# One layer of a hybrid decoder on one core: the MLP's products by one level of Strassen's scheme

## The chip, the core and the metric

The kernel runs on one core of a Trainium2 chip. The core has five engines, each with its own instruction queue, worked off in order: TensorE (PE, matrix products, results in PSUM), VectorE (DVE), ScalarE (ACT), GpSimd (POOL) and SyncE (SP), which here only issues transfers between memory and SBUF. The metric is the device time of one execution in microseconds. Before the change it is 2307.84 us (median of 3 runs, 2306.13 to 2308.58).

## The reference, cut to what matters

```
h   = layer_norm(x)                       # x: 2048 tokens x 1024
z   = h @ w_in                            # input projection, 2320 columns
mix = concat(s5(z), gla(z), rglru(z)) @ w_out
h   = layer_norm(2**0.25 * h + mix)
ff  = square(relu(h @ mlp_w1)) @ mlp_w2   # 1024 -> 4096 -> 1024
out = layer_norm(2**0.25 * h + ff)
```

All arrays are float32. The three mixers and the input projection are not touched by the change.

## The kernel before, in words

The order of every engine's work is written out by hand: the kernel builds a list of ticks (`tick`, L211), each with some matrix products of TensorE, and spreads everything else over the ticks; the emission loop (L1617) then issues it all in program order. No compiler reorders it.

A float32 product is made of three matmuls: each operand is split into a high part (a ScalarE copy to float32r) and the rest (a VectorE subtraction), and `mm3` (L219) adds high x high, high x low and low x high. One matmul has 128x128 weights and 512 moving columns. Weights come from memory in pieces, are split by `stage_weights` (L1508, ScalarE at L1526, then VectorE; instructions that an engine helper records have line 77, and those of `mm3` L221 to L223) and used at once.

After the input projection, whose ticks also hold the mixers, the 2048 tokens go in two halves of 1024 (blocks 0 and 1, then 2 and 3, of 512 tokens). For each half: the out-projection of its two blocks (`add_out_proj`, L1253, 32 ticks of 12 matmuls, banks `po`), the residual and the first LayerNorm (`ln1`, L1279), transposes of the rows through TensorE (`h1t`, L1287, `tp_h1T`), and the MLP (`add_mlp`, L1299). The MLP takes the hidden layer in blocks of 256 columns: `p1` makes 128 hidden columns for 512 tokens with 24 matmuls (banks `pz_ph`), ScalarE and VectorE apply relu and square and split the result (`hid`), and `p2` adds the block's part of the second product (banks `pf`) to the rows, which stay in SBUF as `acc`, by one VectorE addition for each bank (`add_acc`, L1338). The hidden layer never leaves SBUF. The last LayerNorm (`ln2_half`, L1408) of the first half lies in the out-projection of the second; that of the second half comes with the last two blocks of the hidden layer. In both the rows' last columns go to ScalarE and GpSimd, the others to VectorE (`NP`, `ln_apply`, L145).

All loads and stores are issued by SP in program order (`load`, L83); an issue waits until its data or its place is ready, and those behind it wait with it.

## Time and profile before

| | |
|---|---|
| median of 3 runs | 2307.84 us |
| profiled execution, span from first to last instruction | 2307.0 us |
| TensorE busy | 2204.8 us, 96%, 10688 matmuls |
| VectorE busy | 1297.4 us, 56% |
| ScalarE busy | 825.9 us, 36% |
| GpSimd busy | 312.9 us, 14% |
| mean granted clock of TensorE | 0.983 |

The profile is of one execution of its own; its span is 0.8 us under the median, and what lies around the span (start and end of the launch) is not in it. Times in a trace are microseconds from the span's start. Idle time is put down to what ended it; for an engine that is not the bottleneck it costs nothing. In a row, `x320` is a count of instructions and `out<-in` names the tiles written and read.

### The profile page before, as it was taken

The numbers are of one execution on the slowest core, as the hardware profiler recorded it, in microseconds if no ns is written. First come the engines' busy times: TensorE is split into PE (matmuls) and PEld (weight loads), VectorE is DVE, ScalarE is ACT, GpSimd is POOL, SyncE is SP. The second block draws the span as 40 slices with busy tenths as digits, with TensorE's granted clock in tenths as the row PEclk, the third lists the DMA queues.
The fourth block names the chain that finished last, engine by engine and source line by source line (L and its number), as shares of the span: only waits on it lengthen the run. The fifth ranks groups of instructions, "written<-read, shape, count | busy, mean of one in ns | idle before, by whom it ended". The sixth has DMA issues, their size and how long they took to land.

```text
span 2307.0 us, 28509 instructions
## 1 busy us (share of the span) xinstructions
PE 2204.8 (96%) x10688; PEld 1840.2 (80%) x10688; DVE 1297.4 (56%) x2210; ACT 825.9 (36%) x1629; POOL 312.9 (14%) x511
## 2 busy tenths in 40 slices
PE   6887999999999999999999999999999999999998
PEld 5776788888877778888888888877788888888886
DVE  5566865546456754445445445967544454454457
ACT  3436656667663332221221222423322212212222
POOL 5486610000002200000000000133000000000003
PEclk9998999999999999999999999999999999999999
DMA  7332354555453331111111113662311111111132
GB/s 208 102 124 77 107 178 119 129 135 135 115 169 107 99 110 55 56 41 51 55 38 55 55 37 102 197 217 69 110 55 55 44 48 55 42 51 55 39 90 105
DMA packets 245130, 212.79 MB, mean 92 GB/s; under 512 B 63856, under 2 KB 196096, under 8 KB 244992
## 3 DMA queue, kind: packets, MB, share of 16 engines
q1 hardware_dynamic: 244224, 208.87, 30.6%
q0 software_dynamic: 768, 2.11, 0.4%
q8 instruction: 84, 1.38, 0.3%
q14 instruction: 54, 0.44, 0.1%
HBM read 174.67 MB, written 36.84 MB: 92 GB/s over the span
## 4 chain that ended last, share of the span: by engine, by line
PE 75%; DVE 9%; POOL 6%; ACT 5%; DMA 2%; issue 2%; SPq 0%; POOLq 0%; DVEq 0%; ACTq 0%
PE pf L223 9%; PE pf L221 9%; PE pf L222 9%; PE pz_ph L222 9%; PE pz_ph L223 9%; PE pz_ph L221 9%; PE po L221 2%; PE po L223 2%; PE po L222 2%; POOL rs_ln L77 1%; POOL rs_in L77 1%; DVE acc L77 1%; PE pr_v L221 1%; PE pr_v L223 1%; PE pr_v L222 1%
## 5 line engine op out<-in xcount | busy, mean ns | idle before, releaser
L221 PE MATMUL pf<-w_w,hid 128*128 128x512 f32 x1024 | 401.7, 392 | 6.8 <-ACT hid L1313 6.8
L223 PE MATMUL pf<-w_w,hid 128*128 128x512 f32 x1024 | 400.8, 391 | 6.8 <-DVE hid L77 6.8
L222 PE MATMUL pf<-w_w,hid 128*128 128x512 f32 x1024 | 400.0, 391 | 1.1 <-DVE w_w L77 1.1
L221 PE MATMUL pz_ph<-act,w_w 128*128 128x512 f32 x1024 | 398.5, 389 | 0.0
L223 PE MATMUL pz_ph<-act,w_w 128*128 128x512 f32 x1024 | 398.4, 389 | 0.0
L222 PE MATMUL pz_ph<-act,w_w 128*128 128x512 f32 x1024 | 398.4, 389 | 0.0
L77 DVE TENSOR_TENSOR acc<-acc,pf 128x512 f32<-128x512 f32 x416 | 281.1, 685 | 173.7 <-PE pf L223 170.6
L1526 ACT ACTIVATE w_w<-st_w 128x512 fp32r<-128x512 f32 x320 | 191.1, 625 | 476.8 <-PE pf L223 425.9
L77 DVE TENSOR_TENSOR rl<-rl 128x512 f32<-128x512 f32 x128 | 92.7, 724 | 425.2 <-ACT hid L1313 425.0
L1312 ACT ACTIVATE rl<-pz_ph 128x512 f32<-128x512 f32 x128 | 76.4, 597 | 470.3 <-PE pz_ph L223 470.2
L77 POOL TENSOR_TENSOR rs_ln<-rs_ln,cst 128x1 f32<-128x1 f32 x32 | 35.7, 1117 | 1470.2 <-DVE rs_ln L77 1469.6
L223 PEld LDWEIGHTS pf<-w_w,hid 128*128 128x128 f32 x1024 | 193.1, 189 | 49.1 <-DVE hid L77 9.0
L221 PEld LDWEIGHTS pf<-w_w,hid 128*128 128x128 f32 x1024 | 193.3, 189 | 47.8 <-ACT hid L1313 8.1
L222 PEld LDWEIGHTS pf<-w_w,hid 128*128 128x128 f32 x1024 | 193.1, 189 | 41.3 <-DVE w_w L77 1.8
L223 PEld LDWEIGHTS pz_ph<-act,w_w 128*128 128x128 f32 x1024 | 192.2, 188 | 40.0
L221 PEld LDWEIGHTS pz_ph<-act,w_w 128*128 128x128 f32 x1024 | 192.2, 188 | 39.8
L222 PEld LDWEIGHTS pz_ph<-act,w_w 128*128 128x128 f32 x1024 | 192.2, 188 | 39.8
L77 DVE TENSOR_TENSOR w_w<-st_w,w_w 128x512 fp32r<-128x512 f32 x320 | 214.0, 698 | 11.5 <-ACT w_w L1526 10.8
L221 PE MATMUL po<-w_wo,act 128*128 128x512 f32 x256 | 104.9, 410 | 7.8 <-DVE acc L77 7.8
L223 PE MATMUL po<-w_wo,act 128*128 128x512 f32 x256 | 102.0, 398 | 0.0
L222 PE MATMUL po<-w_wo,act 128*128 128x512 f32 x256 | 101.7, 397 | 0.0
L77 DVE TENSOR_TENSOR hid<-rl,hid 128x512 fp32r<-128x512 f32 x128 | 88.5, 691 | 4.4
(358 smaller groups left out, 3442.7 us busy)
## 6 DMA issues: line engine op xcount, KB each, us to landing
st_w<-in_mlp_w_dram SPq DMA_DIRECT2D x320, 256.0 KB, 3.0
st_wo<-in_w_out_dram SPq DMA_DIRECT2D x64, 256.0 KB, 3.1
w<-s5w_d SPq DMA_DIRECT2D x16, 640.0 KB, 5.1
xr<-in_x_dram SPq DMA_DIRECT2D x16, 512.0 KB, 5.1
h_d<-xr SPq DMA_DIRECT2D x16, 512.0 KB, 4.5
mx<-mix_d SPq DMA_DIRECT2D x16, 512.0 KB, 5.4
acc<-h_d SPq DMA_DIRECT2D x16, 512.0 KB, 5.2
out_dram<-acc SPq DMA_DIRECT2D x12, 512.0 KB, 4.3
```

The costliest lines, as they stand in the source:

```text
L77: return fn(*a, **k)
L221: T.matmul(ps, lhs[0], rhs[0], start=first, stop=False)
L222: T.matmul(ps, lhs[0], rhs[1], start=False, stop=False)
L223: T.matmul(ps, lhs[1], rhs[0], start=False, stop=last)
L1312: S.activation(rl, ps, AF.Relu)
L1526: S.activation(u.tile[:, 0], st, AF.Copy)
```

## The change: what it does

Strassen's scheme (in Winograd's form) computes a product of 2x2 blocks with 7 block products in place of 8, at the price of sums of blocks before and after.

The four out-projection blocks now follow each other, then comes the whole MLP. Rows after `ln1` are stored to memory (`h1_d`). Jobs (`tjob`) load them, transpose them, form the 7 right operands of MLP 1 with ScalarE, VectorE and GpSimd, and store them (`rop_d`): 16 jobs for tokens 0 to 1023 during the out-projection, 16 more during MLP 1.

MLP 1 has 32 steps: 1024 tokens x 256 hidden columns each, 16 steps for each half of the tokens. A step has 7 products of 12 matmuls; the right operands of a half stay in SBUF (7 rings of 1 MB in memory, split once). Left operands are sums of blocks of `mlp_w1`, made by GpSimd and then split. Two or three products are added in one bank after the other, with copies (ScalarE) of the bank in between; relu and square give four blocks of the hidden layer, from which GpSimd makes sums, and 7 operands go to memory (`hid_d`).

MLP 2 has 64 parts: 8 chunks of 512 hidden rows, and in each 8 parts of 256 tokens. A part has 7 products of 6 matmuls. Its left operands are loaded from `hid_d` and split, its right ones are sums of blocks of `mlp_w2`, made and split once in a chunk. Results are added to the rows of all tokens, which lie in SBUF (`acc`, 8 tiles of 256 tokens): four additions by VectorE from PSUM, three by GpSimd from ScalarE's copies. The last LayerNorm of a tile follows its last chunk.

`V`, `G`, `S`, `T` are VectorE, GpSimd, ScalarE, TensorE; `task(n, ...)` puts work behind product n of `run`, and `evac` handles the product before.

```diff
+    o0 = len(plan)
+    hooks["op", 0] = o0
+    for b in range(4):
+        add_out_proj(b)
+    def h1_ready(b, t):
+        if t % 2:
+            z["h1", b // 2, 2 * (b % 2) + t // 2] = True
+    for t in range(4):
+        for b, n in ((1, o0 - 2), (2, o0 + 17), (3, o0 + 33)):
+            hook(n + 2 * t, mix_load, b, 2 * t)
+            hook(n + 2 + 2 * t, mix_split, b, 2 * t)
+        for b in range(4):
+            hook(o0 + 16 * b + 2 + t, acc_load, b, t)
+        for b in range(3):
+            n = o0 + 16 * b + 16 + 2 * t
+            hook_two(n, ln1, b, t, NP[4 + b % 2])
+            hook(n + 3, h1_ready, b, t)
+    hook(o0 + 1, set_gb, "gb1", ln1_g[0], ln1_b[0], "ln1")
...
-                z["accp"] = open_pool("accp", bufs=8)
+                z["accp"] = open_pool("accp", bufs=6)
                 z["gbp"] = open_pool("gbp")
-            if n == hooks["mlp", 0]:
+                z["tjp"] = open_pool("tjp")
...
+        gens = [ln1(3, t, NP[5]) for t in range(4)]
+        for g in gens:
+            next(g)
+        for g in gens:
+            for _ in g:
+                pass
+            for e in late:
+                e()
+            late.clear()
+        drain("tj0")
+        for nm in ("tjp", "gbp", "accp", "psp", "smallp", "wst", "rowp", "wp", "actp", "const"):
+            close_pool(nm)
...
+        ORDER = ("p1", "p2", "p7", "p6", "p3", "p4", "p5")
+        INDEX = {"p1": 0, "p2": 1, "p7": 2, "p6": 3, "p4": 4, "p5": 5, "p3": 6}
...
+        def split(dst_hi, dst_lo, src):
+            S.activation(dst_hi, src, COPY)
+            V.tensor_tensor(dst_lo, src, f(dst_hi), op=ALU.subtract)
...
+            def products(g, p):
+                nonlocal last
+                i = INDEX[p]
+                if p == "p1":
+                    g.bank["a"] = ps2.tile([P, BLK], F32, tag="a", name=f"pa_{g.nm}", bufs=3)
+                elif p == "p2":
+                    g.bank["b"] = ps2.tile([P, BLK], F32, tag="b", name=f"pb_{g.nm}", bufs=2)
+                elif p == "p7":
+                    g.bank["c"] = ps2.tile([P, BLK], F32, tag="c", name=f"pc_{g.nm}", bufs=2)
+                ps = g.bank["b" if p == "p2" else "c" if p in ("p7", "p4") else "a"]
+                terms = g.terms(i)
+                for k, (lhs, rhs) in enumerate(terms):
+                    mm3(ps, lhs, rhs, k == 0 and p in ("p1", "p2", "p7"), k == len(terms) - 1,
+                        p not in ("p1", "p2", "p7"))
+            def evac():
+                nonlocal last
+                if last is not None:
+                    last[0].evac(last[1])
+                last = None
+            for g in groups:
+                for p in ORDER:
+                    for e in tasks.pop((n, "before"), ()):
+                        e()
+                    who = prev if p == "p3" else g
+                    if who is not None:
+                        products(who, p)
+                    evac()
+                    if who is not None:
+                        last = who, p
+                    for e in tasks.pop(n, ()):
+                        e()
+                    n += 1
+                prev = g
+            evac()
+            products(prev, "p3")
+            prev.evac("p3")
...
+        def ring_load(sb, i):
+            rt = rings[sb][i] = ringp.tile([P, 2, 4, BLK], F32R, tag=f"ring{i}", name=f"ring_{sb}_{i}")
+            load(f(rt[:, 1]), rop_d[sb, i].rearrange("k p c -> p k c"))
+        def ring_split(sb, i, hf):
+            rt = rings[sb][i]
+            ks = slice(2 * hf, 2 * hf + 2)
+            split(rt[:, 0, ks], rt[:, 1, ks], f(rt[:, 1, ks]))
...
+            def load(self):
+                self.raw = raw_tile([P, KD, 2, P], f"w1_{self.nm}")
+                load(self.raw, w1_v[:, :, 256 * self.c:256 * self.c + 256].rearrange("p k (i c) -> p k i c", i=2))
...
+            def sum(self, which):
+                a = self.a
+                if which == 1:
+                    a["s1"] = sump.tile([P, 4, P], F32, tag="s1", name=f"s1_{self.nm}")
+                    G.tensor_tensor(a["s1"], a["21"], a["22"], op=ALU.add)
...
+            def keep(self, i, nm):
+                store(hid_d[self.sb, self.c, i], self.out[nm])
+            def copy(self, nm, ps):
+                self.out[nm] = t = cpp.tile([P, BLK], F32, tag=nm if nm == "p1" else "pu", name=f"{nm}_{self.nm}",
+                                            bufs=1 if nm == "p1" else 2)
+                S.activation(t, ps, COPY)
+            def add(self, i, nm, ps, other):
+                t = self.tile(nm)
+                V.tensor_tensor(t, ps, self.out[other], op=ALU.add)
+                V.scalar_tensor_tensor(t, t, 0.0, t, op0=ALU.max, op1=ALU.mult)
+                self.keep(i, nm)
+            def evac(self, p):
+                bank = self.bank
+                if p == "p1":
+                    self.copy("p1", bank["a"])
+                elif p == "p2":
+                    self.add(0, "c11", bank["b"], "p1")
+                elif p == "p7":
+                    self.copy("p7", bank["c"])
+                elif p == "p6":
+                    self.copy("u2", bank["a"])
+                elif p == "p4":
+                    self.add(1, "c21", bank["c"], "u2")
+                elif p == "p5":
+                    self.add(4, "c22", bank["a"], "p7")
+                else:
+                    t = self.tile("c12")
+                    S.activation(t, bank["a"], AF.Relu)
+                    S.activation(t, t, AF.Square)
+            def hsum(self, which):
+                o = self.out
+                if which == 1:
+                    G.tensor_tensor(self.tile("s1"), o["c12"], o["c22"], op=ALU.add)
+                    self.keep(5, "s1")
...
+        steps = [Step(n) for n in range(32)]
+        steps[0].load()
+        steps[1].load()
+        for i in range(7):
+            ring_load(0, i)
+        for w in (1, 3, 2):
+            steps[0].sum(w)
+        def first(i):
+            steps[0].split(i)
+            if i == 1:
+                steps[0].sum(4)
+            for hf in range(2):
+                ring_split(0, i, hf)
+        first(0)
...
+        for i, n in ((2, 0), (3, 1), (4, 2), (5, 3), (6, 5)):
+            task(n, first, i)
+        for n in range(31):
+            m = steps[n + 1]
+            b = 7 * n
+            if n:
+                task(b - 7, m.load)
+            o = 4 if n == 0 else 0
+            for w, k in ((1, 0), (3, 0), (2, 1)):
+                task(b + max(k, o), m.sum, w)
+            for i, k in ((0, 0), (1, 1)):
+                task(b + max(k, o), m.split, i)
+            task(b + max(2, o), m.sum, 4)
+            for i, k in ((2, 2), (3, 3), (4, 4), (5, 6), (6, 6)):
+                task(b + max(k, o), m.split, i)
+        for n in range(32):
+            for w, k in ((1, 5), (3, 6), (2, 6), (4, 7)):
+                task(7 * n + 7 + k, steps[n].hsum, w)
+        for i, k in enumerate((0, 1, 2, 3, 5, 6, 11)):
+            task(7 * 15 + k, ring_load, 1, i)
+            for hf in range(2):
+                task(7 * 15 + k + 5, ring_split, 1, i, hf)
...
+            def split(self, i):
+                nm = ("11", "21", "t3", "t2", "t4", "t1", "22")[i]
+                t = w2p.tile([P, 2, 2, 512], F32R, tag="b22" if i == 6 else "b", name=f"w2o_{self.c}_{i}",
+                             bufs=2 if i == 6 else 8)
+                self.op[i] = t
+                for j in range(2):
+                    split(t[:, 0, j], t[:, 1, j], self.b[nm, j])
...
+        chunks = [Chunk(c) for c in range(8)]
+        task(7 * 31 + 3, chunks[0].load)
+        run(steps, tasks)
+        for nm in ("cp", "tjp2", "ringp", "sump", "smp"):
+            close_pool(nm)
...
+            def load(self):
+                self.t = accq.tile([P, 2, D], F32, tag=f"acc{self.g}", name=f"accq_{self.g}")
+                load(self.t, h1_d[256 * self.g:256 * self.g + 256, :].rearrange("(i p) c -> p i c", p=P))
+            def scale(self):
+                S.activation(self.t, self.t, COPY, scale=ALPHA)
...
+            def ln(self, i):
+                st = smalls.tile([P, 2, 6], F32, tag="lnst", name=f"st2_{self.g}_{i}")
+                r = self.t[:, i]
+                for c in range(2):
+                    V.bn_stats(st[:, c, :], r[:, c * 512:(c + 1) * 512])
+                mv = smalls.tile([P, 2], F32, tag="lnmv", name=f"mv2_{self.g}_{i}")
+                V.bn_aggr(mv, st)
+                rs = self.rs = smalls.tile([P, 3], F32, tag="lnrs", name=f"rs2_{self.g}_{i}")
+                V.tensor_scalar(rs[:, 0:1], mv[:, 1:2], LN_EPS, None, op0=ALU.add)
+                G.tensor_tensor(rs[:, 1:2], rs[:, 0:1], mhalf_c, op=ALU.pow)
+                V.scalar_tensor_tensor(rs[:, 2:3], mv[:, 0:1], -1.0, rs[:, 1:2], op0=ALU.mult, op1=ALU.mult)
+            def ln_apply(self, i):
+                r, rs = self.t[:, i], self.rs
+                g_t, b_t = z["gb2"]
+                tok = 256 * self.g + P * i
+                S.activation(r, r, AF.Identity, scale=rs[:, 1:2], bias=rs[:, 2:3])
+                V.tensor_tensor(r, r, g_t, op=ALU.mult)
+                for c in range(2):
+                    cs = slice(512 * c, 512 * c + 512)
+                    (V if c else G).tensor_tensor(r[:, cs], r[:, cs], b_t[:, cs], op=ALU.add)
+                    store(of[tok:tok + P, cs], r[:, cs])
...
+            def load(self):
+                self.raw = hrp.tile([P, 7, 2, P], F32, tag="hr", name=f"hr_{self.nm}", bufs=2)
+                sb, tt = divmod(self.n % 8, 4)
+                for j in range(2):
+                    load(self.raw[:, :, j, :],
+                         hid_d[sb, 2 * self.ch.c + j, :, :, tt * P:tt * P + P].rearrange("o p c -> p o c"))
+            def split(self, i):
+                no = 1 if i == 3 else 2
+                t = sm2.tile([P, 2, no, 2, P], F32R, tag="h4" if i == 3 else "h", name=f"ho_{self.nm}_{i}",
+                             bufs=2 if i == 3 else 4)
+                self.op[i] = t
+                split(t[:, 0], t[:, 1], self.raw[:, 2 * i:2 * i + no])
...
+            def add(self, nm, E, src):
+                d = self.acc.at(nm)
+                E.tensor_tensor(d, d, src, op=ALU.add)
+            def evac(self, p):
+                bank = self.bank
+                if p == "p1":
+                    self.p1 = self.copy(bank["a"], "p1")
+                elif p == "p2":
+                    self.add("c11", V, bank["b"])
+                    self.add("c11", G, self.p1)
+                elif p == "p7":
+                    self.add("c22", G, self.copy(bank["c"], "p7"))
+                elif p == "p6":
+                    self.add("c21", G, self.copy(bank["a"], "u2"))
+                elif p == "p4":
+                    self.add("c21", V, bank["c"])
+                elif p == "p5":
+                    self.add("c22", V, bank["a"])
+                else:
+                    self.add("c12", V, bank["a"])
...
+        parts[0].load()
+        parts[1].load()
+        for g in range(8):
+            acc[g].load()
+        parts[0].split(0)
+        chunk0(0)
+        chunk0(1)
+        parts[0].split(1)
+        acc[0].scale()
...
+        for n in range(63):
+            m = parts[n + 1]
+            b = 7 * n
...
+            for i, k in ((0, 0), (1, 2), (2, 4), (3, 5)):
+                task(b + (max(k, 4) if n == 0 else k), m.split, i)
+            if n + 2 < 64:
+                task(b + 6, parts[n + 2].load)
+        for g in range(1, 8):
+            task(7 * (g - 1) + 3, acc[g].scale)
+        for c in range(7):
+            ch = chunks[c + 1]
+            b = 56 * c
+            task(b + (8 if c == 0 else 1), ch.load)
+            for j in range(2):
+                task(b + 14 + 3 * j, ch.sum, 3, j)
+                task(b + 20 + 3 * j, ch.sum, 1, j)
+                task(b + 33 + 3 * j, ch.sum, 2, j)
+                task(b + 39 + 3 * j, ch.sum, 4, j)
+            for i, k in ((6, 27), (0, 29), (1, 31), (2, 50), (3, 51), (4, 52), (5, 53)):
+                task(b + k, ch.split, i)
...
+        for g in range(8):
+            n = 7 * (56 + g)
+            for i, k in ((0, 13), (1, 15)):
+                task(n + k, acc[g].ln, i)
+                task(n + k + 1, acc[g].ln_apply, i)
+        run(parts, tasks)
```

## Rows read from the trace of the kernel before

**Rows 1.** The page: busy time of each engine; granted clock in 40 slices.
```profile
PE 2204.8 (96%) x10688; PEld 1840.2 (80%) x10688; DVE 1297.4 (56%) x2210; ACT 825.9 (36%) x1629; POOL 312.9 (14%) x511
...
PEclk9998999999999999999999999999999999999999
```

**Rows 2.** The page: the chain that ended last, share by engine, by line.
```profile
PE 75%; DVE 9%; POOL 6%; ACT 5%; DMA 2%; issue 2%; SPq 0%; POOLq 0%; DVEq 0%; ACTq 0%
PE pf L223 9%; PE pf L221 9%; PE pf L222 9%; PE pz_ph L222 9%; PE pz_ph L223 9%; PE pz_ph L221 9%; PE po L221 2%; PE po L223 2%; PE po L222 2%; POOL rs_ln L77 1%; POOL rs_in L77 1%; DVE acc L77 1%; PE pr_v L221 1%; PE pr_v L223 1%; PE pr_v L222 1%
```

**Rows 3.** Busy time by stage: stretch, length, engines, granted clock, DMA share, GB/s.
```profile
655.00:777.00 122.00, 110.99 (x536) 90.56 (x535) 74.09 (x133) 52.78 (x122) 20.82 (x23) 0.97 0.46 142
777.00:870.00 93.00, 85.66 (x374) 69.08 (x374) 60.63 (x92) 34.77 (x60) 17.53 (x20) 0.96 0.31 95
870.00:1450.00 580.00, 580.00 (x2560) 480.26 (x2559) 286.05 (x436) 133.92 (x223) 1.54 (x1) 1.00 0.19 57
...
2260.00:2307.00 47.00, 35.53 (x157) 29.10 (x155) 35.03 (x58) 9.99 (x16) 18.94 (x22) 0.93 0.25 95
```

**Rows 4.** Timeline of TensorE in MLP 1, the first and last of 46.
```profile
1689.71 0.39 PE L222 MATMUL pz_ph<-act,w_w 128*128 128x512 f32 x1
...
1699.91 0.39 PE L222 MATMUL pz_ph<-act,w_w 128*128 128x512 f32 x1
```

**Rows 5.** Timeline: four transposes of rows, one after the other.
```profile
1620.57 1.06 PE L171 MATMUL tp_h1T<-ident,acc 128*128 128x128 f32 x4
```

**Rows 6.** GpSimd's groups by form: busy, mean ns, idle before.
```profile
L77 POOL TENSOR_TENSOR rs_ln<-rs_ln,cst 128x1 f32<-128x1 f32 x32 | 35.7, 1117 | 1470.2 <-DVE rs_ln L77 1469.6 <-DVE ss L77 0.6
...
L77 POOL TENSOR_TENSOR acc<-acc,b_ln 128x384 f32<-128x384 f32 x12 | 14.5, 1212 | 0.9
...
L77 POOL TENSOR_TENSOR rs_ln<-rs_ln 128x1 f32<-128x1 f32 x20 | 13.2, 660 | 1.7
...
L77 POOL TENSOR_TENSOR acc<-acc,g_ln 128x384 f32<-128x384 f32 x12 | 12.1, 1007 | 9.8 <-ACT acc L158 9.8
...
L77 POOL TENSOR_TENSOR acc<-acc,g_ln 128x512 f32<-128x512 f32 x8 | 10.3, 1292 | 6.5 <-ACT acc L158 6.5
...
L77 POOL TENSOR_SCALAR rs_ln<-mv_ln 128x1 f32<-128x1 f32 x20 | 8.0, 400 | 0.0
```

**Rows 7.** Busy time by stage: the stretch with the most DMA traffic.
```profile
670.00:680.00 10.00, 9.95 (x51) 8.45 (x52) 5.03 (x9) 4.80 (x16) 1.01 (x1) 1.00 0.97 334
```

**Rows 8.** DMA issues: count, KB each, median us from issue to landing.
```profile
out_dram<-acc SPq DMA_DIRECT2D x4, 192.0 KB, 1.9
```

**Rows 9.** Groups by form, VectorE and ScalarE.
```profile
L77 DVE TENSOR_TENSOR acc<-acc,pf 128x512 f32<-128x512 f32 x416 | 281.1, 685 | 173.7 <-PE pf L223 170.6
L77 DVE TENSOR_TENSOR w_w<-st_w,w_w 128x512 fp32r<-128x512 f32 x320 | 214.0, 698 | 11.5 <-ACT w_w L1526 10.8
...
L77 DVE BATCH_NORM_STATS2 st_ln<-acc 128x6 f32<-128x512 f32 x32 | 20.4, 680 | 0.0
...
L77 DVE TENSOR_TENSOR act<-mx,act 128x1024 fp32r<-128x1024 f32 x16 | 19.6, 1223 | 20.6 <-ACT act L1123 20.6
...
L1526 ACT ACTIVATE w_w<-st_w 128x512 fp32r<-128x512 f32 x320 | 191.1, 625 | 476.8 <-PE pf L223 425.9 <-PE pz_ph L223 21.5 <-DVE acc L77 16.4
...
L1123 ACT ACTIVATE act<-mx 128x1024 fp32r<-128x1024 f32 x16 | 16.9, 1058 | 42.2 <-DMA mx<-mix_d 42.2
```

**Rows 10.** Timeline in an out-projection: GpSimd and VectorE beside each other.
```profile
1546.61 1.30 POOL L77 TENSOR_TENSOR acc<-acc,g_ln 128x512 f32<-128x512 f32 x1 [0.93 <-ACT acc L158]
1547.08 1.37 DVE L77 TENSOR_TENSOR w_wo<-st_wo,w_wo 128x512 fp32r<-128x512 f32 x1 [1.45 <-ACT w_wo L1526]
1547.98 1.62 POOL L77 TENSOR_TENSOR acc<-acc,b_ln 128x512 f32<-128x512 f32 x1
```

**Rows 11.** Timeline in MLP 1, beside a GpSimd addition.
```profile
1617.67 1.53 DVE L77 TENSOR_TENSOR rl<-rl 128x512 f32<-128x512 f32 x1 [1.97 <-ACT hid L1313]
```

**Rows 12.** Timeline of TensorE: the last matmul.
```profile
2295.14 0.39 PE L223 MATMUL pf<-w_w,hid 128*128 128x512 f32 x1
```

419 lines of the change are left out of this document (235 added, 184 removed).

## The prediction, made before the change was built or timed

> **What bounds the kernel now.** I read the page's busy line and clock slices first, then the chain of waits, then the busy time by stage, then the TensorE timeline inside a stage, then durations by form. TensorE is busy 96% of the span at full clock, VectorE 56%, ScalarE 36%, GpSimd 14% [rows 1]. The chain that ended last is three quarters TensorE, and of that the six matmul lines of the MLP (pf and pz_ph) are 54% of the span [rows 2]. By stage: from 870 to 1450 us TensorE is busy in every microsecond; it has gaps at 655 to 777 (out-projection of blocks 0 and 1 with the mixers' rest), at 777 to 870, and in the last 47 us [rows 3]. Inside the MLP one matmul starts every 10.20/45 = 0.2267 us [rows 4]; this pitch, not the 0.39 us that one lasts, prices a matmul. So in the MLP fewer matmuls is less time, one for one, as long as nothing else becomes late. The execution's span is 2307.0 and the median of the runs 2307.84, so I work in the span and add 0.8.
>
> **What goes.** The MLP has 2 halves x 32 tiles of hidden columns x 2 blocks x 24 matmuls, and as many in the second product: 6144. After: 32 steps of 7 products of 12 matmuls (2688), then 64 parts of 7 products of 6 (2688), together 5376. 768 fewer x 0.2267 = 174 us. A product is 2.72 us in a step (a step 19.04) and 1.36 in a part (a part 9.52).
>
> **Up to the end of the out-projection.** Everything up to 777 stays in its order; I cost it at nothing (bounds -5 and +10: block 2's splits and the transposing jobs now share that stretch with the mixers). Blocks 2 and 3 follow at once: 384 x 0.2267 = 87, about 40 transposes at 1.06/4 = 0.26 [rows 5] = 10, and 4 for a VectorE that now does a LayerNorm in each block: E = 878, end of the last out-projection (870 to 892).
>
> **Seam 1, out-projection to MLP 1.** Nothing is left for TensorE until MLP 1 has operands, and these loads stand on SP's queue behind the stores of block 3's rows, which wait for its LayerNorm. VectorE has its first statistics at E+2.5 (0.9 for the last sum, 1.6 for statistics); GpSimd then does four times 1.12 + 0.40 + 0.66 = 8.7 and four times 1.01 + 1.21 = 8.9 [rows 6], so SP is free at E+20. Behind it are 2 weight loads and 7 ring loads of 1.05 MB each. The best stretch of the trace moves 334 GB/s [rows 7], 3.14 us each, and 2 us pass before the first lands (a 192 KB store takes 1.9 [rows 8]). Ring 0 lands at E+31.4, ring 5, which the sixth product needs, at E+47.1; its two splits take 1.06 + 2 x 1.22 [rows 9], the last matmuls 1.4: step 0 ends at E+52, and I add 2 for the clock (granted 0.93 on average in the 47 us with the longest gaps, and 1.00, which is 2.4 GHz, without gaps [rows 3]). Its six products are 16.3 us of work, so the seam costs 38 (25 to 50).
>
> **MLP 1.** Per step ScalarE has 12 operations of 0.62 (7.5), VectorE 13 of 0.69 (9.0; 14.6 if each GpSimd operation holds one up by 0.7, see MLP 2), GpSimd 8 of 1.29 (10.3) [rows 6, 9], beside 19.04 of TensorE. SP's loads are issued a whole step ahead; the stores ahead of them wait for GpSimd, but only for work of one product before. Covered, then: 2616 matmuls = 593, 64 transposes = 16, and 4 where the seven rings are reloaded in step 15 (7.3 MB plus 2.9 MB of other traffic take 31 us at 334 GB/s; each ring has 7 products, 19 us, and the next product's splits as slack). F = 878 + 54 + 613 = 1545, end of MLP 1. If the cover fails by 1 us a step it is 32.
>
> **Seam 2, MLP 1 to MLP 2.** Part 0's load is on SP behind the stores of the last hidden sums: two ScalarE operations to F+1.5, then four GpSimd sums of 1.29, F+6.7. Two part loads (0.92 MB, 2.75 us) and then eight accumulator loads of 1.05 MB are queued. ScalarE, in order, splits part 0 (F+11.5), splits weights, and at F+17.8 scales accumulator 0 (landed F+17.4) in 1.9 (2048 columns, by the slope from 512 to 1024 [rows 9]). Behind this are six weight splits, three copies and a split, 10 x 0.62, before the last two products: part 0 ends at F+28.8. Part 2's load lies behind all accumulators: (10.2 + 0.92) MB / 334 GB/s + 8.7 = F+42. ScalarE reaches its split at F+29 and waits; queued behind is the copy of part 1's first product, without which TensorE cannot add the fourth into that bank. It goes on at F+43.5 with 9 products (12.2 us) done: cost 31 (18 to 45).
>
> **MLP 2, steady.** Per part: ScalarE three copies, 3.5 splits and one eighth of a chunk's 14, 8.25 x 0.625 = 5.2; VectorE four adds of 0.685 from PSUM and the same 5.25 splits, together 6.4 [rows 9]; GpSimd three adds and on average one weight sum, 4 x 1.29 = 5.2 [rows 6], beside 9.52 of TensorE. The cover is not free: beside GpSimd operations, VectorE operations with two SBUF operands took longer in this trace. One that else lasts 0.69 took 1.37 beside a GpSimd operation, and the next GpSimd one 1.62 where the first took 1.30 [rows 10]; another of that size took 1.53 [rows 11]. I walk a part, from its start, a product every 1.36: product 2 is done at 2.9, VectorE adds it and makes a split (ready since ScalarE's half at 3.6) to 4.3; GpSimd's add of product 1 runs 4.2 to 5.4, that of 7 to 6.7, that of 6, copied by 6.2, to 8.0. The split that ScalarE has ready at 6.9 waits until 8.0; the adds of products 3, 4 and 5 end at 9.2, 10.3 and 11.0, the next part's first split at 11.7, 0.7 before that part's own product 2. TensorE asks for the bank that was read at 11.0 only at 9.5 + 5.4. So two of the four GpSimd operations meet a VectorE operation of this kind, 0.7 each: 6.4 + 1.4 = 7.8, and TensorE sets the pace. At each change of a chunk VectorE has 8 splits within 4 products and runs some 4 us late (1.5 on TensorE), and 2.1 MB of weights stand before a part load (2): 3.5 x 6 = 21 (0 to 60). Part 58 starts at 1545 + 43.5 + (58 x 42 - 54 =) 2382 x 0.2267 + 21 = 2149.5.
>
> The Trainium skill, SBUF — State Buffer, "Who interferes with whom", says that VectorE with two SBUF inputs and a GpSimd instruction that reads SBUF exclude one another, the later one blocked until the first is through. The trace agrees with 1.37 and 1.62. By that rule the two share one part's 9.52 with 5.2 + 5.25 x 0.69 = 8.8, where the walk above has 7.8 of VectorE alone; rival 1 is that rule made the bound.
>
> **LayerNorm 2.** Now all 16 row tiles fall in the last of eight chunks, two a part from part 57's end. For one, VectorE has two statistics (1.3 [rows 9]), two small operations (0.4), a wait for GpSimd's power (1.12 and 0.1), one more small one (0.2), a product of 1024 columns (1.22), half a sum (0.69): 5.0. Two and the part's own 5.2 are 15.2; to these come four waits: the product of 1024 columns for GpSimd's add of product 1 (1.1), the third split for GpSimd's half sum (1.1), the fourth for its add of product 7 (0.5), and VectorE's add of product 4 for GpSimd's of product 6 into the same rows (1.1): 19. VectorE, in order, then sets the pace, as TensorE needs its splits: from part 58, 3 + 6 x 19 - 3.5 (no splits after the last), 1.4 for the last sums, 1.9 + 3 x 6.2 for the tiles left (each with 1.2 for ScalarE), 1.2 and a store of 2.3: 138, where six parts of TensorE are 57. Cost 81; bounds 44 (13 a part, no waits) and 95. Before, the same stretch had 11.9 from the last matmul's start at 2295.1 to the end [rows 12].
>
> Sum: 2149.5 + 138 = 2287.5 span, 2288 us as run. Against before: -174, +38 +31 +21 +81, less what before lost in gaps of its own.
>
> **Rivals.**
> 1. VectorE becomes the clock of all of MLP 2 (slower). It decides from 9.52 - 6.44 = 3.1 us of blocking a part, 0.77 for each of four GpSimd operations. For: single collisions of 0.68 and 0.84 [rows 10, 11]; if VectorE is always behind, each collides. Against: nearly half of VectorE's time is adds from PSUM and small idle stretches. Price: with the full 1.29, 6.4 + 5.2 = 11.6, 2.1 x 56 = 118, less the 21 already counted: 2385; with 1.0 a part is 10.4: 2317. Taken as 2350.
> 2. Seams and LayerNorm at their low ends: LayerNorm 2 at 13 to 15 us a part (-30), the rings in time (-10), the chunk changes hidden (-12): 2235. For: DMA and ScalarE have room, and waits on the lock may fall in VectorE's other waits. Against: in-order queues put them one behind the other.
> 3. The gain is eaten exactly: E ten later, seam 2 at 40: 2307, no change.
>
> The count of products itself is not in doubt: it follows from the loops.
>
> **How the numbers follow.** Forecast (2288, own range 2258 to 2315) 0.57, rival 1 0.21, rival 2 0.14, rival 3 0.08. Under 0.2% (4.6 us) a measurement of this kernel can't tell from no change. Of the forecast 0.46 lies under 2303, 0.04 within, 0.07 over; rival 3 gives 0.06 to the same and 0.02 to slower. Faster 0.60, same 0.10, slower 0.30. The range leaves out the ends of rivals 1 and 2: 2230 to 2350.
>
> **What would show it.** Right: 0.227 us from matmul to matmul in both layers; TensorE idle some 30 us at about 880, with a stretch of rings behind; idle about 14 and again 10 us near 1545, the second ending with a part load; VectorE over 90% busy or waiting on GpSimd in the last 130 us while TensorE is at a half. Wrong: MLP 2 parts longer than 10 us in the middle (rival 1), TensorE waiting in MLP 1 for a GpSimd sum, a last chunk at TensorE's pace (rival 2), or the end of the out-projection far from 878.

## The result, and the profile after

The changed kernel takes 2371.23 us (median of 4 runs, 2369.17 to 2373.76) against 2307.39 of the kernel before on the same chip: a ratio of 1.0279, 95% interval 1.0264 to 1.0293. It is 2.8% slower; the forecast was 2288 and faster, and the time is outside its range (2258 to 2315, with the rivals 2230 to 2350). The profiled execution has a span of 2368.7 us.

The page of the changed kernel, busy time and granted clock, to be held against [rows 1]:

```profile
PE 2086.6 (88%) x9920; PEld 1717.7 (73%) x9920; DVE 1560.6 (66%) x2302; ACT 1063.7 (45%) x2077; POOL 1153.3 (49%) x1087
...
PEclk9998999999999889799999999998999999999987
```

TensorE has 768 matmuls fewer, as forecast, and 118 us less busy time, not 174: its mean granted clock went from 0.983 to 0.950. Its idle time went from 102 to 282 us. Where, the stages show (stretch in us, length, busy time of each engine with its count, granted clock, DMA share, GB/s):

```profile
655.00:777.00 122.00, 98.94 (x463) 79.33 (x461) 73.72 (x127) 50.14 (x117) 24.72 (x29) 0.94 0.55 177
777.00:870.00 93.00, 66.96 (x256) 51.93 (x256) 43.73 (x74) 21.58 (x46) 30.61 (x40) 0.85 0.65 196
...
1050.00:1300.00 250.00, 237.86 (x1048) 194.39 (x1048) 168.87 (x182) 89.82 (x170) 162.63 (x124) 0.98 0.56 178
...
1400.00:1600.00 200.00, 200.00 (x885) 165.58 (x884) 145.82 (x138) 73.53 (x126) 134.26 (x86) 1.00 0.44 152
...
1700.00:2200.00 500.00, 493.16 (x2150) 401.26 (x2149) 363.87 (x500) 248.71 (x452) 318.58 (x207) 1.00 0.41 120
2200.00:2300.00 100.00, 78.21 (x306) 60.99 (x305) 80.72 (x121) 39.45 (x65) 48.89 (x36) 0.91 0.35 103
```

From 777 to 870 TensorE starts 256 matmuls where it started 374 [rows 3], and no other engine is even half busy: a stretch of waits. MLP 1 has gaps in its first half and none from 1400 to 1600; MLP 2 is at TensorE's pace from 1700 to 2200. The borders of the stages are read from the matmuls by the bank that they write (po is the out-projection, pa_s MLP 1, pa_m MLP 2); a row gives min/median/max of the duration and the first and last start:

```profile
L235 PE MATMUL po<-w_wo,act x256: 387/389/632, 656.3 to 939.8; 128*128 128x512 f32 x128
...
L233 PE MATMUL pa_s<-ring,w1o_s x512: 387/389/795, 974.4 to 1636.2; 128*128 128x512 f32 x171
...
L235 PE MATMUL pa_s<-ring,w1o_s x512: 387/389/628, 976.2 to 1636.7; 128*128 128x512 f32 x171
L233 PE MATMUL pa_m<-w2o,ho_m x512: 387/389/796, 1650.8 to 2342.2; 128*128 128x512 f32 x171
...
L235 PE MATMUL pa_m<-w2o,ho_m x512: 388/389/628, 1652.2 to 2343.1; 128*128 128x512 f32 x171
```

| step of the forecast | forecast | measured | difference |
|---|---|---|---|
| E, end of the out-projection | 878 | 939.8 | +62 |
| first product of MLP 1 | E+32.5 | E+34.6 | +2 |
| F, end of MLP 1 | E+667 | E+696.9 | +30 |
| first product of MLP 2 | idle about 14 | F+14.1 | 0 |
| end of the program | F+742.5 | F+732.0 | -10 |

62 + 30 - 10 is 82, and 2287.5 + 82 = 2369 is the span. (E+32.5 is the landing of ring 0 at E+31.4 and ScalarE's 1.06.)

What fills the out-projection is seen in its timeline. A transposing job reads two h1 tiles (tjr), transposes them on TensorE, makes seven operands of them on ScalarE, VectorE and GpSimd (tjo) and stores them (rop_d). This is one period of it (start, duration, engine; in brackets the idle time before and what ended it; lines of other work left out):

```profile
771.99 0.39 ACT L1322 ACTIVATE tjo<-tjp 128x256 f32<-128x256 f32 x1 [4.69 <-DMA rop_d<-tjo]
...
772.42 0.63 ACT L1420 ACTIVATE w_wo<-st_wo 128x512 fp32r<-128x512 f32 x1
...
773.00 1.32 POOL L74 TENSOR_TENSOR tjo<-tjo 128x128 f32<-128x128 f32 x2 [5.39 <-DVE tjo L74]
...
774.35 0.37 SPq L81 DMA_DIRECT2D rop_d<-tjo  x1
...
774.82 1.53 SPq L81 DMA_DIRECT2D tjr<-h_d  x2
...
778.77 0.38 ACT L1322 ACTIVATE tjo<-tjp 128x256 f32<-128x256 f32 x1 [5.71 <-DMA rop_d<-tjo]
...
779.21 0.63 ACT L1420 ACTIVATE w_wo<-st_wo 128x512 fp32r<-128x512 f32 x1
```

ScalarE waits 5.7 us until the store of the job before has landed, since tjo has one buffer; the next split of out-projection weights (w_wo) is queued behind that wait, so in this stretch TensorE gets one set of weights, 12 matmuls, in 6.8 us where it could use one every 2.7 (12 x 0.2267). The sums of these waits from 655 to 940 us (ScalarE's largest, then TensorE's largest; us in total, times, longest):

```profile
ACT tjo L1322 <- DMA rop_d<-tjo: 79.7, 14, 7.7
```

```profile
PE tjp L1318 <- DVE tjo L74: 28.2, 12, 4.5
```

### The profile page after: what moved, and what is told of

It reads as the page before. It is cut to its first block, busy times and chain, and to the rows that moved or that the text cites. A ratio compares the mean times of both kernels' runs of the same rounds, so it can differ in the third digit from the quotient of the medians.

```text
span 2368.7 us, 29132 instructions
## 1 busy us (share of the span) xinstructions
PE 2086.6 (88%) x9920; PEld 1717.7 (73%) x9920; DVE 1560.6 (66%) x2302; ACT 1063.7 (45%) x2077; POOL 1153.3 (49%) x1087
## 3 DMA queue, kind: packets, MB, share of 16 engines
q0 software_dynamic: 768, 2.11, 0.4%
## 5 line engine op out<-in xcount | busy, mean ns | idle before, releaser
L74 DVE TENSOR_TENSOR ho_m<-hr_m,ho_m 128x512 fp32r<-128x512 f32 (+1 forms) x256 | 217.8, 852 | 148.6 <-ACT ho_m L1624 148.6
L74 POOL TENSOR_TENSOR accq<-accq,p_m 128x512 f32<-128x512 f32 x128 | 196.8, 1553 | 218.0 <-DVE accq L74 211.5
L233 PE MATMUL pa_m<-w2o,ho_m 128*128 128x512 f32 x512 | 209.1, 408 | 55.3 <-ACT p_m L1966 28.1
L74 DVE TENSOR_TENSOR w1o_s<-w_s,w1o_s 128x512 fp32r<-128x512 f32 x160 | 204.7, 1294 | 58.2 <-ACT w1o_s L1624 58.2
L233 PE MATMUL pa_s<-ring,w1o_s 128*128 128x512 f32 x512 | 204.4, 399 | 39.3 <-ACT ring L1624 34.2
L1624 ACT ACTIVATE ho_m<-hr_m 128x512 fp32r<-128x512 f32 (+1 forms) x256 | 142.8, 574 | 184.3 <-PE pa_m L235 79.5
L234 PE MATMUL pa_s<-ring,w1o_s 128*128 128x512 f32 x512 | 203.7, 398 | 3.3 <-DVE ring L74 3.3
L234 PE MATMUL pa_m<-w2o,ho_m 128*128 128x512 f32 x512 | 204.9, 400 | 0.0
L235 PE MATMUL pa_m<-w2o,ho_m 128*128 128x512 f32 x512 | 203.8, 398 | 0.0
L235 PE MATMUL pa_s<-ring,w1o_s 128*128 128x512 f32 x512 | 203.0, 396 | 0.0
L233 PEld LDWEIGHTS pa_m<-w2o,ho_m 128*128 128x128 f32 x512 | 99.4, 194 | 89.7 <-ACT p_m L1966 33.9
L1624 ACT ACTIVATE w1o_s<-w_s 128x512 fp32r<-128x512 f32 x160 | 99.8, 625 | 123.7 <-PE pa_s L235 43.9
L233 PEld LDWEIGHTS pa_s<-ring,w1o_s 128*128 128x128 f32 x512 | 98.5, 192 | 60.9 <-ACT ring L1624 34.6
L234 PEld LDWEIGHTS pa_s<-ring,w1o_s 128*128 128x128 f32 x512 | 98.3, 192 | 25.8 <-DVE ring L74 5.7
L235 PEld LDWEIGHTS pa_m<-w2o,ho_m 128*128 128x128 f32 x512 | 99.2, 194 | 21.4
L234 PEld LDWEIGHTS pa_m<-w2o,ho_m 128*128 128x128 f32 x512 | 99.3, 194 | 20.5 <-DVE w2o L74 0.8
L235 PEld LDWEIGHTS pa_s<-ring,w1o_s 128*128 128x128 f32 x512 | 98.3, 192 | 21.0 <-DVE w1o_s L74 0.2
L233 PE MATMUL pc_m<-w2o,ho_m 128*128 128x512 f32 x256 | 101.2, 395 | 10.8 <-ACT p_m L1966 7.7
```

Source lines behind the costliest of these rows:

```text
L74: return fn(*a, **k)
L233: T.matmul(ps, lhs[0], rhs[0], start=first, stop=False, skip_group_check=more)
L234: T.matmul(ps, lhs[0], rhs[1], start=False, stop=False, skip_group_check=more)
L235: T.matmul(ps, lhs[1], rhs[0], start=False, stop=last, skip_group_check=more)
L1624: S.activation(dst_hi, src, COPY)
```

## The experiments

Every kernel below is the changed kernel with one edit, unless it says otherwise. E, the two ends of MLP 1 and of MLP 2 are read as in the rows above. Among the runs that leave the out-projection as it is, E lies between 935.5 and 941.9, so E is good to some 3 us; a single time is good to about 3 us too.

### Is it the jobs, and which part of them?

**The jobs moved behind the out-projection.** Edit: the line that starts the 16 jobs goes from the out-projection's first tick to behind its last product.

```
-                active.append(tjob_ticks([(0, i) for i in range(16)]))
...
+        active.append(tjob_ticks([(0, i) for i in range(16)]))
         drain("tj0")
```

> The 16 transposing jobs of the first half stand behind the out-projection, where nothing overlaps them; the computation is whole. Theory A (the 62 us by which the out-projection ends late come from the jobs between its products): the last product starts at 868 to 885 in place of 939.8; then 16 jobs alone, at the 6.7 us that one took before, are about 107 us, so that MLP 1 begins near 1010 to 1030 and the time is 2405 to 2430. Theory B (they come from VectorE's sums into the accumulators, from the LayerNorms on GpSimd, or from the clock, whatever the jobs do): the last product still starts after 920 and the time is above 2450.

2410.78 us. The out-projection of that kernel:

```profile
L235 PE MATMUL po<-w_wo,act x256: 388/389/632, 657.5 to 884.1; 128*128 128x512 f32 x128
```

E = 884.1: theory A. Between the products the jobs cost 56 us. The forecast had given them 10, for their transposes, so 46 of the 62 us are theirs. Without these 10 it would have said 868, so 16 us lie elsewhere. Some 6 of them come before 777 us, by which time this kernel has 357 of the out-projection's matmuls where the kernel before has 383; behind 777 the trace names two waits of TensorE for VectorE's sums (9.5 us, where the forecast had 4 for VectorE). No run takes these 16 apart.

**More output buffers.** Edit: once GLA's buffers are free (tick 32 of the out-projection), tjo comes from a pool with three.

```
-        ot = pool.tile([P, 7, P], F32, tag="tj_o", name=f"tjo_{nm}")
+        ot = (z.get("tjx") or pool).tile([P, 7, P], F32, tag="tj_o", name=f"tjo_{nm}", bufs=3 if z.get("tjx") else 1)
...
                 close_pool("glap")
+                z["tjx"] = open_pool("tjx", side="right")
```

> From the second block on, the jobs' output tile has three buffers in place of one; nothing else differs. Theory A1 (a job's first ScalarE copy waits for the job before to land in DRAM, and ScalarE's weight splits queue behind it): the waits of tjo on rop_d (79.7 us, 14 times) go, the last product starts at 880 to 900, the time falls by 40 to 60 us to 2310 to 2330. Theory A2 (the jobs cost by their own work on VectorE, GpSimd, the one transposing bank and the order of SP's queue): the last product starts after 920 and the time is within 20 us of 2371.

2354.28 us (ratio to before 1.0200, 1.0183 to 1.0217), E = 922.2: by its words that is theory A2 (after 920, and 17 us under 2371). But the edit reaches only jobs 8 to 15, because the first eight are issued before tick 32: these stood 6.5 us apart, about as before, and the others 4.6 in place of 6.9. So the next kernel gives two buffers from the first job on, the second a slot for weights.

```
-        ot = pool.tile([P, 7, P], F32, tag="tj_o", name=f"tjo_{nm}")
+        wpool, wtag = z["wslot"] if sb == 0 and i % 2 else (pool, "tj_o")
+        ot = wpool.tile([P, 7, P], F32, tag=wtag, name=f"tjo_{nm}", bufs=1)
...
                 z["tjp"] = open_pool("tjp")
+                z["wslot"] = free.pop()
```

> Three buffers from the second half of the jobs on took 17.6 us off the out-projection, but the first eight jobs still stood on one buffer there. Here jobs alternate between that buffer and one weight slot from the first job on, one job a tick as before. Theory A1 (the waits on the store of the job before are the cost): the 6.7 us between first copies fall to 3 to 4.5 us for all 16 jobs, and the last product starts at 895 to 910 (in place of 939.8). Theory A2 (one transposing bank, SP's order and the jobs' own work): still above 920.

2343.53 us; the out-projection and TensorE's and SP's rows of that kernel:

```profile
L235 PE MATMUL po<-w_wo,act x256: 387/389/628, 657.5 to 914.5; 128*128 128x512 f32 x128
```

```profile
PE tjp L1318 <- DMA tjr<-h_d: 18.4, 9, 7.1
```

```profile
765.62 0.36 SPq L81 DMA_DIRECT2D rop_d<-tjo  x1
766.08 1.54 SPq L81 DMA_DIRECT2D tjr<-h_d  x2
...
769.30 0.37 SPq L81 DMA_DIRECT2D rop_d<-tjo  x1
```

E = 914.5, 25 us less and 4.5 above what A1 expected; the first copies are 4.9 us apart in the first eight jobs and 4.6 in the others, not 3 to 4.5. The wait for the store is gone, and the next one of the same chain is in its place: SP issues the next job's loads right behind this job's store, which waits for GpSimd's sums, and TensorE's transposes wait for those loads.

**Pacing, then loads ahead.** Both on top of the two buffers. In the first a job starts every second tick. In the second also the transposes come two ticks after the loads, so that the loads are queued ahead of the store; its lines:

```
-            if todo and ("h1", todo[0][0], todo[0][1] // 4) in z:
+            if todo and rest <= 0 and len(running) < 2 and ("h1", todo[0][0], todo[0][1] // 4) in z:
...
+                rest = 2
...
-            ready = running[:-1] if fresh else running
-            if ready and ready[0][1] == 1:
+            if running and running[0][1] == 1 and t - running[0][2] >= 2:
```

> As the run before, and a job begins every second tick in place of every tick, so that the 16 jobs spread over the second to fourth block. Theory A3 (what is left beyond the buffer is that jobs come in two bunches, faster than a chain of load, transposes, copies, sums and store can pass): the last product starts at 882 to 895, 10 to 20 us below the run without pacing. If the jobs' own work is the cost, pacing changes nothing (within 5 us).

2345.39 us, E = 918.5: pacing alone changes nothing. A3, my theory of bunches, is wrong; TensorE's waits for the loads grew to 27.4 us in 20 waits.

> In the out-projection, two output buffers from the first job on, a job every second tick, and each job's loads two ticks ahead of its transposes, so that the next job's loads stand in SP's queue ahead of the store of this one (in the run with pacing alone they stood behind it and the last product started at 918.5). Theory A4 (the chain store, next loads, landing, transposes, copies, sums, next store is what is left): the last product starts at 885 to 900 and TensorE's 27.4 us of waits on these loads go. If the jobs' own work or the DMA share is left: 910 or more.

2322.68 us; the out-projection:

```profile
L235 PE MATMUL po<-w_wo,act x256: 387/389/632, 654.5 to 895.6; 128*128 128x512 f32 x128
```

```profile
PE tjp L1318 <- DMA tjr<-h_d: 11.4, 4, 4.5
```

E = 895.6: theory A4, though 11.4 us of the waits stay. E is now taken apart: 25 us are the output buffer (939.8 to 914.5), 19 the order of loads and stores on SP (to 895.6, with the pacing; the loads ahead alone were not run), 11.5 what the jobs still cost (to 884.1; the forecast had 10), and 16 what is late without any job (to 868).

### MLP 1: jobs or sums?

**The second half's jobs left out; the sums left out.** Edits: the 48 tasks of the jobs go and ring 1 is loaded from half 0 (shown); or every `G.tensor_tensor` of `Step.sum` and `Step.hsum` goes.

```
-            task(n, tj, i, 0)
-            task((n + 3, "before"), tj, i, 1)
-            task(n + 3, tj, i, 2)
...
-            load(f(rt[:, 1]), rop_d[sb, i].rearrange("k p c -> p k c"))
+            load(f(rt[:, 1]), rop_d[0, i].rearrange("k p c -> p k c"))
```

> The 16 jobs of the second half inside MLP 1 are left out: its second ring is loaded from the first half's operands, so that the second half of the output is computed from the wrong rows; all else runs. MLP 1 took 662 us from first to last product. Theory C (its 30 us too many are TensorE's waits on the jobs' loads and copies, 14.4 us by the waits, and the clock that falls with them): 625 to 638 us, the time 2340 to 2350. Theory D (VectorE's splits at 1.29 us beside GpSimd's sums delay TensorE): 650 us or more, the time 2358 or more.

> GpSimd's eight sums a step are left out of MLP 1 (operands stand in for them, so the output is not the reference's); stores, splits and products are as many as before. Theory D (the sums stretch VectorE's splits from 0.70 to 1.29 us and that delays TensorE): the splits are back at about 0.70 us and MLP 1 takes 630 to 640 us in place of 662. Theory C (the jobs of the second half do it): the splits get shorter and MLP 1 still takes 650 us or more.

2343.23 and 2340.64 us; MLP 1 from first to last product takes 631.8 and 635.6 us in place of 662.3. Each theory is borne out by its own run, so neither is whole: it takes both. VectorE's weight splits in MLP 1, with the sums and without them (busy us, mean ns, then idle time before):

```profile
L74 DVE TENSOR_TENSOR w1o_s<-w_s,w1o_s 128x512 fp32r<-128x512 f32 x158 | 201.8, 1291 | 47.8 <-ACT w1o_s L1624 47.8
```

```profile
L74 DVE TENSOR_TENSOR w1o_s<-w_s,w1o_s 128x512 fp32r<-128x512 f32 x223 | 150.1, 687 | 164.8 <-ACT w1o_s L1624 162.7 <-PE tjp L1318 2.0
```

A split is 0.60 us longer on average beside the sums (what the prediction calls the lock), and not evenly so. Shortest, median and longest in the changed kernel:

```profile
L74 DVE TENSOR_TENSOR w1o_s<-w_s,w1o_s x159: 676/1769/1786, 976.6 to 1615.0; 128x512 fp32r<-128x512 f32 x159
```

Over half of the splits take some 1.1 us more, others next to nothing more; without the sums all lie between 682 and 695 ns. But the run without jobs had the long splits too (1313 ns on average), and its MLP 1 was no slower than that of the run without sums. The sums act through their stores, as a timeline of the changed kernel shows:

```profile
1115.03 1.71 POOL L74 TENSOR_TENSOR s_s<-s_s,w_s 128x512 f32<-128x512 f32 x1
1115.09 0.32 SPq L81 DMA_DIRECT2D hid_d<-s_s  x1
1115.50 0.93 SPq L81 DMA_DIRECT2D tjr<-h_d  x2
...
1119.71 0.83 PE L1318 MATMUL tjp<-ident,tjr 128*128 128x128 f32 x4 [3.87 <-DMA tjr<-h_d]
```

The loads of a job leave SP right after the store of a sum that GpSimd has just finished, and TensorE, which has to do the transposes before its next product, stands 3.87 us. Hence the test: the same loads, four products earlier.

```
-            task(n, tj, i, 0)
+            task(n - 4, tj, i, 0)
```

> Inside MLP 1 each job's two loads are issued 7 block products ahead of its transposes in place of 3; nothing is left out. Leaving the jobs out took 30.5 us off MLP 1's 662 us, and leaving the sums out 26.7 us, which can't both be their own work. Theory CD (the loads stand in SP's queue behind stores that wait for GpSimd's slow sums, so TensorE's transposes wait for them): 630 to 640 us from first to last product, the time near 2345. Theory C alone (the jobs' transposes and copies themselves): 655 us or more.

2345.44 us; MLP 1's first and last products:

```profile
L233 PE MATMUL pa_s<-ring,w1o_s x512: 387/389/796, 971.5 to 1611.6; 128*128 128x512 f32 x171
...
L235 PE MATMUL pa_s<-ring,w1o_s x512: 387/389/628, 973.4 to 1612.1; 128*128 128x512 f32 x171
```

640.6 us, 21.7 less with all the work done: the order on SP, not the work. TensorE waits no more on tjr in that stage; the jobs' own 9 us (to 631.8) are less than the 16 of the forecast. The other 8 of the 30 us were not tested; in this kernel TensorE still waits 8.5 us in five waits for the splits of the reloaded rings, where the forecast had 4, and once 4.2 us for a copy in the first step. Whether sums of 1.29 us would have come in time, no run shows.

### The seams

Edits: block 3's h1 stores are issued by GpSimd; accumulators 1 to 7 are loaded one a part.

```
+        out = nc.gpsimd.dma_start if b == 3 else store
...
-        for g in range(8):
-            acc[g].load()
+        acc[0].load()
...
         for g in range(1, 8):
-            task(7 * (g - 1) + 3, acc[g].scale)
+            task(7 * (g - 1) + 1, acc[g].load)
+            task(7 * (g - 1) + 5, acc[g].scale)
```

> Two edits at different places, each read in its own stretch. First seam: the four stores of the last block's rows are issued from GpSimd's queue, so that SP goes on to the loads for MLP 1 while the LayerNorm runs. If SP's order bounds the seam, MLP 1's first product starts 10 to 22 us after the last out-projection product in place of 34.6; if the LayerNorm or the space of the operands bounds it, 30 us or more. Second seam: the accumulators' loads of groups 1 to 7 are spread over the first seven parts, so that part 2's hidden operands don't stand behind 8 MB. If SP's order bounds it, MLP 2 from its first to its last product takes 680 to 686 us in place of 692.3; if the bandwidth does, 690 or more.

2356.66 us. MLP 1's first matmul starts 12.7 us after E in place of 34.6, so SP's order did bound the start. The Trainium skill (DMA: Bandwidth & Descriptors, "Issuing engines are not separate DMA queues") has it that issuing from several engines saves only the sequencer's time; here it saved 22 us of a wait, since a sequencer that waits for one store holds all that is queued behind. But 13 us came back at once: TensorE's waits from 905 to 1000 us in that kernel,

```profile
PE pa_s L233 <- ACT ring L1625: 12.3, 1, 12.3
PE pa_s L234 <- DVE ring L74: 10.1, 2, 9.5
```

show the second matmul waiting for VectorE, which has block 3's LayerNorm queued ahead of the ring's low half. From E to F it is 688.4 us in place of 696.9: 8 gained.

MLP 2 takes 690.7 us from first to last product in place of 692.3. That is no difference: kernels that leave MLP 2 alone have 689.3 to 696.0. SP's rows show why. The first two are of the changed kernel (its wait from 1640 to 1680 us, and the issue of part 2's load), the third is the same issue in the kernel with the spread loads:

```profile
SPq L81 <- DVE ho_m L74: 12.0, 1, 12.0
...
1669.53 0.97 SPq L81 DMA_DIRECT2D hr_m<-hid_d  x2
```

```profile
1656.85 0.97 SPq L81 DMA_DIRECT2D hr_m<-hid_d  x2
```

Both leave 18.7 us after MLP 2's first product (1650.8 and 1638.2). Part 2's load does not wait for the accumulators' loads but for VectorE's splits of part 0, since the raw operands (hr) have two buffers.

### The last pass

The changed kernel's chain of waits in the last pass (the longer of the pieces that release one another, start and duration; one of four rounds like it):

```profile
2254.95 1.21 DVE st L74 x2
2257.43 1.25 ACT accq L1928
2258.71 2.11 DVE accq L74
2261.45 1.79 DVE ho_m L74
2264.05 5.01 DMA hr_m<-hid_d
2269.67 1.23 ACT accq L1928
2270.93 1.24 DVE accq L74
...
2272.88 1.21 DVE st L74 x2
```

One part takes 18.3 us (from one pair of statistics to the same one of the next part: (2309.66 - 2236.57)/4), and the forecast said 19. But 5 us of it are a load that the forecast did not have. Four edits went at it. The first three change the LayerNorm alone: the small multiply of VectorE at the head of the second step; three steps; the multiply on GpSimd, with ScalarE's scaling a product later.

```
-                V.scalar_tensor_tensor(rs[:, 2:3], mv[:, 0:1], -1.0, rs[:, 1:2], op0=ALU.mult, op1=ALU.mult)
+                stt(G, rs[:, 2:3], mv[:, 0:1], -1.0, rs[:, 1:2], ALU.mult, ALU.mult)
...
-                task(n + k + 1, acc[g].ln_apply, i)
+                task(n + k + 2, acc[g].ln_scale, i)
+                task(n + k + 3, acc[g].ln_apply, i)
```

(These are the third's lines; in the first and second the line that goes stands again at the head of `ln_apply` or `ln_scale`, and in the second the two steps are one and two products after the sums.)

> In the last LayerNorm VectorE's small multiply by GpSimd's power stands at the head of the second step in place of the end of the first, so that VectorE doesn't wait there; all else as before. If VectorE bounds the last pass: 16 waits of about 1.1 us go and the time falls by 12 to 19 us to 2352 to 2359. If GpSimd's sums or the last chain of stores bound it: within 4 us of 2371.

> The last LayerNorm in three steps, one block product apart: sums and power, then the small multiply and ScalarE's scaling, then VectorE's and GpSimd's gamma and beta. With two steps the wait for GpSimd went and 20.9 us of waits for ScalarE took its place. If these waits bound the last pass: the time falls by 8 to 18 us to 2353 to 2363. If it is bound by VectorE's and GpSimd's own work and the rate at which products come: within 4 us of 2371.

> The last LayerNorm alone is changed: the small multiply goes to GpSimd, right behind its power; ScalarE's scaling is issued two block products after the sums in place of one, gamma and beta three. In the two versions that only moved the multiply on VectorE, ScalarE waited 56 to 67 us for VectorE's small results and the copies of products stood behind it (TensorE waited 36 us for those copies). If ScalarE's place in that order bounds the last pass: its waits on the small results fall below 20 us, MLP 2's products end 10 to 25 us sooner after F, and the time is 2346 to 2362. If VectorE's work bounds it: within 5 us of 2371.

2371.60, 2379.40 and 2368.99 us: none of the three gains. In the first two VectorE's waits for GpSimd's power fell from 11.0 us to 2, and its waits for ScalarE grew from 7.1 to 20.9; in the third ScalarE's waits for VectorE's or GpSimd's small results fell from 55.8 to 39.5, and those for hidden operands grew from 34.8 to 51.1. SP's rows show what else is there (the changed kernel, 2200 to 2330 us; then its timeline):

```profile
SPq L81 <- POOL accq L74: 91.4, 11, 14.8
```

```profile
2256.12 7.39 SPq L81 DMA_DIRECT2D out_dram<-accq  x4
2263.60 1.11 SPq L81 DMA_DIRECT2D hr_m<-hid_d  x2
```

Four output stores hold SP for 7.4 us, and the next part's operands leave right behind: once more a load behind stores that wait. The fourth edit issues the stores 7 products later.

```
-                    store(of[tok:tok + P, cs], r[:, cs])
+            def out(self, i):
+                tok = 256 * self.g + P * i
+                for c in range(2):
+                    cs = slice(512 * c, 512 * c + 512)
+                    store(of[tok:tok + P, cs], self.t[:, i, cs])
...
                 task(n + k + 1, acc[g].ln_apply, i)
+                task(n + k + 8, acc[g].out, i)
```

> In the last pass the output stores of each row block are issued 7 block products after its gamma and beta instead of with them, so that they stand in SP's queue behind the next part's loads of hidden operands; the LayerNorm itself is untouched. In the chain of waits of the changed kernel these loads start right behind stores that wait for GpSimd (SP waited 91.4 us for it from 2200 to 2330 us, ScalarE's splits 34.8 us for the loads). If that order bounds the last pass: those 34.8 us fall below 12, from the first to the last product of MLP 2 it takes 662 to 682 us in place of 692.3, and the time is 2341 to 2361. If VectorE's work bounds it: within 5 us of 2371.

2367.24 us: 4 less, not 10 to 30. The load has left the chain (ScalarE's waits, 2200 to 2370 us), and others are in its place:

```profile
ACT accq L1928 <- DVE rs L74: 78.8, 16, 8.0
...
ACT ho_m L1624 <- DMA hr_m<-hid_d: 1.7, 1, 1.7
```

So the load and ScalarE's wait for small results lay beside each other: where an edit shortens the one, the other grows (to 51.1 with the third edit, from 55.8 to 78.8 here). The last run below has both edits.

### Do the terms add?

The two cures of the jobs together (two buffers, pacing and loads ahead in the out-projection; loads ahead in MLP 1); the same with both seams and the third LayerNorm edit; the same with both seams and the late stores; all of it.

> The two cures for the jobs together: in the out-projection two output buffers, a job every second tick and loads two ticks ahead; in MLP 1 loads seven block products ahead. Alone they took 44 us off the last out-projection product and 22 us off MLP 1. If both act on different stretches and nothing gives them back: 2371 - 44 - 22 = 2305, 2298 to 2312, no change against the kernel before. If one gives the other's gain back (a later ring, the clock, DMA): above 2315.

> The same with the first seam's stores on GpSimd's queue, the accumulators' loads spread, and the last LayerNorm as in the run of that edit alone. The first seam gave back most of its 22 us and kept 8, the second kept 2. If the terms add: 2305 - 8 - 2 - (0 to 25 for the LayerNorm) = 2270 to 2297, faster than both kernels. If the LayerNorm isn't bound as thought: 2290 to 2300.

> Both cures of the jobs (2304.6 together), both seam edits (8 and 2 us), and the late stores of the last pass. If the terms add: 2304.6 - 10 - (10 to 30) = 2264 to 2285. If the last pass is bound by VectorE after all: 2290 to 2297.

> As the run before, with the last LayerNorm's small multiply on GpSimd and ScalarE's scaling a block product later. If ScalarE's place is what is late once the loads come in time: 3 to 12 us below the run before. If VectorE is: within 3 us of it, or slower, as that edit alone was worth 2 us.

| run | us | against before, ratio (95%) |
|---|---|---|
| cures of the jobs | 2304.59 | 0.9986 (0.9977 to 0.9995) |
| cures + seams + third LayerNorm edit | 2298.57 | 0.9955 (0.9941 to 0.9969) |
| cures + seams + late stores | 2294.50 | 0.9949 (0.9933 to 0.9966) |
| cures + seams + late stores + third LayerNorm edit | 2283.06 | 0.9897 (0.9882 to 0.9912) |

The cures add as expected: 2305 expected, 2304.59 measured. The second and third rows miss my ranges by 1.6 and 9.5 us and lie where the alternative put them: of the two edits of the last pass one alone gains nearly nothing. The fourth row is 11.4 us below the third. Read in its own stretch, from MLP 2's first product to the end of the span, the four kernels have 717.2, 720.2, 715.2 and 701.6 us; kernels that leave this stretch alone have 715.0 to 721.3. So neither edit alone is clear of that spread, and both together take some 15 us off. How long a part of the last pass takes says the same, and so do TensorE's waits for the copies of products (p_m, last 169 us):

| last pass | us a part | TensorE's waits for p_m, us |
|---|---|---|
| changed kernel | 18.3 | 33.3 |
| third LayerNorm edit alone | 20.4 | 33.8 |
| late stores alone | 17.3 | 25.8 |
| both (fourth row above) | 16.3 | 4.3 |

The fourth version beats the kernel before by 1.0% and the changed one by 3.7%. This is its stretch that begins 549 us after MLP 2's first product, as 2200 to 2300 does in the changed kernel:

```profile
2127.00:2227.00 100.00, 81.35 (x325) 61.90 (x323) 90.53 (x124) 42.99 (x69) 64.34 (x57) 0.94 0.39 117
```

VectorE is at 91% where it had 81%, TensorE at 81% where it had 78%. So VectorE, the bound of the last pass by the forecast, is near to being it once the other two waits are gone.

## Why the prediction was wrong, point by point

- **The count of matmuls and the pitch** (-174): right. 1400 to 1600 and 1700 to 2200 run at 0.226 and 0.23 us a matmul.
- **Up to the end of the out-projection, "384 x 0.2267 = 87, about 40 transposes ... = 10, and 4 for a VectorE that now does a LayerNorm in each block: E = 878": the step that failed**, and the largest miss, 62 us. I priced the jobs by what TensorE does for them and did not walk their chain: load, transposes, copies, sums, store, with one output buffer and one queue. Jobs can follow one another through that chain every 6.7 us, and one is issued every tick of 2.7; 44 us went away when the chain was opened, with every job still done. In all the jobs cost 56 us where the sum has 10 for them. The other 16 us of the miss are "Everything up to 777 stays in its order; I cost it at nothing", which was some 6 us late even without jobs, and TensorE's waits for sums behind it; their cause stays open. The bounds of 870 to 892 left it out because the tick's other work was priced as if nothing were queued behind a job's wait.
- **MLP 1, "SP's loads are issued a whole step ahead"**: true of the weights, not of the jobs' loads, which come three products ahead and behind the stores of sums. 22 of the 30 us are this. The next clause, that the stores wait "only for work of one product before", was wrong in the same place: SP waited up to 8.3 us for one sum (974 to 1300 us), three products, and most sums last 1.63 to 1.74 us, not 1.29. The other 8 of the 30 stay open.
- **Seam 1**: right in mechanism and size (E+34.6, and SP's order was what held it).
- **Seam 2**: right up to the first product (F+14.1). Behind it "Part 2's load lies behind all accumulators" was wrong: the load waits for its buffer. That ScalarE reaches the split at F+39.7, near the forecast's F+43.5, is luck, and TensorE idles 0.24 us there, not 10, because it comes late itself after other waits (1.9, 3.1 and 2.5 us) and at the lower clock.
- **MLP 2, steady**: right; rival 1, VectorE as its clock, did not happen. VectorE is 73% busy and TensorE 98.6%. From 1677.6, where the second seam ends with nine products done, to part 58 at 2230.0 (2429 matmuls since 1650.8) it is 552 us, 14 more than the matmuls' pitch gives, where the forecast had 21 for the chunk changes; this and 2.6 us of seam 2 are the -10 from F on. The Trainium skill's rule (SBUF — State Buffer, "Who interferes with whom") is borne out by 1291 against 687 ns. It did not make VectorE the clock here; in the last pass it is on the chain itself (below).
- **LayerNorm 2**: the size is right (138.7 us from part 58 to the end against 138, though the terms add up to 138.9; 18.3 us a part against 19), and that is partly luck. Two of the four waits for GpSimd are seen on the chain, about 1 us each (VectorE's product of 1024 columns takes 2.11 us in place of 1.24, a split 1.79 in place of 0.69). But 5 us are a load behind output stores, which the forecast did not have, and VectorE is about 80% busy, not the only bound.
- **Rivals 2 and 3**: neither. That E could be late by 62 us I named as a sign of error and gave no rival.
